# Two rings for the small statistics tiles of a hybrid encoder block

## The chip, the cores and the metric

The kernel runs on one core of a Trainium2 chip. The metric is the time of one execution on the device in microseconds; less is better. The tables and rows come from one profiled execution, taken by the hardware profiler: busy times of TensorE (PE, and PEld for its weight loads), VectorE (DVE), ScalarE (ACT), GpSimd (POOL) and the queue of SyncE (SP), which here issues DMAs only.

## The reference

One layer: an RMS norm and one input projection feed three token mixers (a gated linear recurrence, "HGRN"; a forgetting attention, "FoX"; a cross-attention into 256 memory tokens); their outputs are projected, gated, summed and projected again. Then follows a convolutional GLU. T = 1024 frames, width 1024, float32. What bears on the change is the query/key norm of the two attentions and the memory attention's softmax:

```python
def _rmsnorm(x, g):
    return xf * lax.rsqrt(jnp.mean(xf * xf, axis=-1, keepdims=True) + EPS) * g
...
    (hq, hf, hi, hg, fq, fk, fv, ff, mq, gate_logits) = jnp.split(z, pts, axis=-1)
...
def _fox_mixer(q, k, v, f_logit, f_bias, q_g, k_g):
    qh = _rmsnorm(q.reshape(B, T, FOX_HEADS, FOX_DH), q_g).transpose(0, 2, 1, 3)
    kh = _rmsnorm(k.reshape(B, T, FOX_HEADS, FOX_DH), k_g).transpose(0, 2, 1, 3)
...
def _memory_mixer(q, mem_kv, q_g, k_g):
    qh = _rmsnorm(q.reshape(B, T, MEM_HEADS, MEM_DH), q_g)
    s = jnp.einsum('bthd,bmhd->bhtm', qh, kh) * (MEM_DH ** -0.5)
    p = jax.nn.softmax(s, axis=-1)
    return jnp.einsum('bhtm,bmhd->bthd', p, vh).reshape(B, T, MEM_WIDTH)
```

## The kernel before, in words

A float32 matrix product is made of three matmuls on a split of each operand into a high and a low part (`mm3`, lines 122 to 124). Large products go by quarters with seven sub-products (Strassen's scheme, Winograd's form); their operands are named `B11`, `B12`, `B21`, `B22`, `T1` to `T4`, each with a high part `h` and a low part `l`.

The part that the change touches is the token-major projection, in five stages. Each is one `tm_unit` (stage 0 is `first_unit`): it takes a 1024 x 512 weight, splits it (`wh`, `wl`), multiplies in the order `B11`, `B21`, `T2`, `T1`, `T3`, `B22`, `T4`, and hands four output tiles `e` to a `put` function. A stage works in three pairs of PSUM banks, `pairs`: one of two `pp`, one of `pp` and `po`, one of two `lg`. Stage 0 makes the memory queries, stage 1 the recurrence's input, stage 2 queries and keys of FoX heads 0 to 3, stage 3 the FoX values, stage 4 queries and keys of heads 4 to 7. Then channel-major units follow (loads `ur`), woven with the FoX attention and the recurrence.

A query/key tile goes through `head_norm`: ACT squares it into the two PSUM banks of a pair (line 608), DVE sums per head (line 609), scales and adds epsilon (line 140), POOL raises to the power -1/2 (line 141), DVE multiplies the tile by it (line 612). Later PE transposes it into the same two banks (line 617), and ACT and DVE split the result into a key tile `ko` (lines 622 and 623), which SP stores. The statistics stand in a tile `r` of at most 16 columns.

Memory attention, `mem_attn`, runs in steps woven into stages 1 and 2 by a list, `slow`; each call of it has two logit steps and two value steps, eight calls in all, so sixteen of each. A logit step: PE logits into a `tr` bank, DVE maximum (line 667), its negative (668), ACT exponential with sum (670), DVE reciprocal (672), POOL scaling of `mpt` (674). The statistics stand in a tile `mst` of 8 columns. A value step: PE transposes of `mpt` (682), a split into `mph` (ACT, line 128) and `mpl` (DVE, line 136), PE products with the values, ACT copy `yo` (690), store. Of `tr` there are two banks, of `mpt` two buffers, of `mph`, `mpl` and `yo` one.

What sets the order: the code is traced in the order in which it is written; a scheduler then lays down one fixed order of instructions for each engine, by the order written, by what each needs, and by when buffers come free. `tm_sum` (line 445) adds weight quarters on POOL. All small tiles come from one place:

```python
def small(name, w):
    return cp.tile([P, 16], F32, tag="small", name=name, bufs=8)[:, :w]
```

This is one ring of eight buffers of 16 columns, with 109 tiles one after the other in it: the four `r` of each of stages 0, 2 and 4, `mst`, a small tile `fb` of the forget logits, the FoX softmax's `st`, and `eg` and `rr` of the recurrence.

Of the kernel before, what the change touches and what calls it, by code (L numbers as in the profile page):

```python
# [9 lines left out]
F32 = mybir.dt.float32  # L10
# [5 lines left out]
P = 128  # L16
# [53 lines left out]
def tile_block(ctx: ExitStack, tc: tile.TileContext, xT, x_rows, memT, mem_rows, vec, fbias, mats, hmask, w_ff, w_tm, w_cm,  # L70
# [4 lines left out]
    cp = ctx.enter_context(tc.tile_pool(name="cp", bufs=1))  # L75
# [22 lines left out]
    lbm, lbe0, lbe1 = (cp.tile([P, 4], F32, tag=t, name=t) for t in ("lbm", "lbe0", "lbe1"))  # L98

    def small(name, w):  # L100
        return cp.tile([P, 16], F32, tag="small", name=name, bufs=8)[:, :w]

    edge = ctx.enter_context(tc.tile_pool(name="edge", bufs=1, side="right"))
    edge.tile([P, EDGE], F32, tag="edge", name="edge")
# [2 lines left out]
    def col(i):  # L107
        return cv[:, i:i + 1]
# [29 lines left out]
    def rstd_small(out, ss, n):  # L138
        w = ss.shape[1]
        V.tensor_scalar(out, ss, 1.0 / n, EPS, ALU.mult, ALU.add)  # L140
        return G.tensor_tensor(out, out, mhalf[:, :w], ALU.pow)
# [427 lines left out]
    def forget_row():  # L569
        fb = small("fb", 2)[:16, :]  # L570
        V.memset(fb, 0.0)
        a, b = (half_tile(f"fr{i}")[:16, :] for i in range(2))
        for n in range(2):
            SP.dma_start(fb[8 * n:8 * n + 8, 0:1], fbias)
            SP.dma_start(a[8 * n:8 * n + 8, :], ffd[:, n * HB:(n + 1) * HB])
        V.tensor_scalar(a, a, fb[:, 0:1], None, ALU.add)
        S.activation(b, a, AF.Abs)
        S.activation(b, b, AF.Sigmoid)
        S.activation(b, b, AF.Ln)
        V.scalar_tensor_tensor(out=b, in0=a, scalar=0.0, in1=b, op0=ALU.min, op1=ALU.add)  # L580
        V.tensor_tensor_scan(a, ones[:16, :].to_broadcast([16, HB]), b, 0.0, ALU.mult, ALU.subtract)
        SP.dma_start(fb[8:16, 1:2], a[0:8, HB - 1:HB])
        V.tensor_scalar(a, a, fb[:, 1:2], None, ALU.add)
        for n in range(2):
            SP.dma_start(negFd[:, n * HB:(n + 1) * HB], a[8 * n:8 * n + 8, :])
# [15 lines left out]
    def head_norm(z, nh, bank):  # L601

        zz = [z[:, 2 * b:2 * b + 2, :].rearrange("p b (h d) -> p (b h) d", h=nh) for b in range(2)]
        r = small(f"r{nh}", 4 * nh)
        rs = [r[:, 2 * nh * b:2 * nh * (b + 1)] for b in range(2)]
        for b in range(2):
            sq = bank[b].rearrange("p (c d) -> p c d", c=2 * nh)
            S.activation(sq, zz[b], AF.Square)
            V.reduce_sum(rs[b], sq, axis=AX.X)
        rstd_small(r, r, 256 // nh)  # L610
        for b in range(2):
            V.tensor_mul(zz[b], zz[b], rs[b].unsqueeze(2).to_broadcast([P, 2 * nh, 256 // nh]))
# [12 lines left out]
    def put_fqk(pp):  # L625
        def put(c, n, z, bank):
            p = 2 * pp + c
            head_norm(z, 4, bank)

            def keys(what):  # L630
                t = ko_tile()
                turned(z, what, col(C_FK) if what == 0 else fqs, (t[:, 0, :], t[:, 1, :]), bank[what])
                SP.dma_start(kqd[p][what][:, :, n * HB:(n + 1) * HB], t.bitcast(F32))
            pending.append(lambda: keys(0))
            pending.append(lambda: keys(1))
        return put

    def put_mq(c, n, z, bank):
        head_norm(z, 2, bank)

        def queries(i):
            h = 2 * c + i
            t = ko_tile()
            turned(z, i, None, (t[:, 0, :], t[:, 1, :]), bank[i])
            SP.dma_start(mqd[h][:, :, n * HB:(n + 1) * HB], t.bitcast(F32))
            attn.append(mem_attn(h, n))
        pending.append(lambda: queries(0))
        pending.append(lambda: queries(1))

    def mem_attn(h, n):  # L650
# [8 lines left out]
        def logits(j):  # L659
            mqh, mql = tiles  # L660
            ps = ps_tr()
            pt = half_tile("mpt").rearrange("p (b m) -> p b m", b=2)
            st = small("mst", 8)
            for b in range(2):
                tsl = slice((2 * j + b) * P, (2 * j + b + 1) * P)
                mm3(ps[:, b * NM:(b + 1) * NM], mqh[:, tsl], mql[:, tsl], mem["mkh"][:, h, :], mem["mkl"][:, h, :], True, True)
            V.reduce_max(st[:, 0:2], ps.rearrange("p (b m) -> p b m", b=2), axis=AX.X)
            V.tensor_scalar(st[:, 2:4], st[:, 0:2], -1.0, None, ALU.mult)
            for b in range(2):
                S.activation(pt[:, b, :], ps[:, b * NM:(b + 1) * NM], AF.Exp, bias=st[:, 2 + b:3 + b],  # L670
                             accum_out=st[:, 4 + b:5 + b])
            V.reciprocal(st[:, 6:8], st[:, 4:6])
            for b in range(2):
                G.tensor_scalar(pt[:, b, :], pt[:, b, :], st[:, 6 + b:7 + b], 0.0, ALU.mult, ALU.add)
            pts.append(pt)
# [868 lines left out]
    for p in range(NF // 2):  # L1544
# [32 lines left out]
        for i in range(2):  # L1577
            f = 2 * p + i
            c = pq.tile([P, T], F32, tag="fc", name="fc", bufs=4)
            w = [col(C_CW + t * NF + f) for t in range(3)]  # L1580
# [88 lines left out]
    for a, b, own, first, c, n, sign, last, xq in (  # L1669
# [9 lines left out]
        for i, ks in enumerate(steps):  # L1679
# [11 lines left out]
            for m in range(4):  # L1691
                w = 256 if end and ks.stop == NP and m == 3 else HB
# [115 lines left out]
```

## Time and profile before

| | |
|---|---|
| median of 3 runs | 1710.43 us (1708.87 to 1712.0) |
| profiled execution, its own time | 1705.72 us |
| its span, first to last instruction | 1704.0 us |
| mean granted clock of TensorE | 0.994 |
| busy: PE, PEld | 1660.5 us (97%), 1417.7 us (83%) |
| busy: DVE, ACT, POOL | 1211.0 us (71%), 844.3 us (50%), 452.7 us (27%) |

Stages 0 to 4 lie between some 56 and 320 us of the span. A matmul counts as busy from its start to its modelled end, and matmuls overlap, so a busy time of PE that is the whole of a stretch means only that one was always in flight; the count of matmuls in the stretch (after the x) tells how fast they went. In timeline rows the columns are start in us, duration in us, engine, line, operation, written tile, read tiles, and in brackets the idle time before with what ended it.

### The profile page before, as it was taken

The page shows a single profiled execution, that of the slowest core. Times are in us where ns is not written, and L with a number is a line of the kernel's source. Part 1 is how long each engine was busy: PE and PEld are TensorE (multiplying, and loading weights), DVE is VectorE, ACT ScalarE, POOL GpSimd, SP SyncE. Part 2 cuts the span into 40 slices and gives each one's busy share as a digit, 9 for nine tenths or more (in the row PEclk, how much of TensorE's full clock was granted, in tenths as well). Part 3 has the DMA queues.
Part 4 walks back from the last instruction along what each step waited for, and adds up shares of the span by engine and source line. Part 5 has one row for each costly group of instructions (what it writes and reads, how often), then busy time and mean ns, then how long its engine had stood idle before and what let it go on. Part 6 is the DMA issues. An engine that isn't in the chain of part 4 may idle for free. (4 is left out here: it accounts for less than half of the span.)

```text
span 1704.0 us, 24944 instructions
## 1 busy us (share of the span) xinstructions
PE 1660.5 (97%) x8883; PEld 1417.7 (83%) x8883; DVE 1211.0 (71%) x2177; ACT 844.3 (50%) x1449; POOL 452.7 (27%) x482
## 2 busy tenths in 40 slices
PE   7999989999999999999999999999999999999999
PEld 5989979977788888888888788788888888888887
DVE  7874565668787676698766767787778878765654
ACT  7745544456666666556432356643434434343432
POOL 1433344365544444323011133311111111100000
PEclk9999989999999999999999999999999999999999
DMA  7352343365564444455966998866445445394772
GB/s 288 110 187 96 108 136 147 125 200 167 174 192 138 146 141 148 161 167 191 317 194 174 300 264 207 227 177 172 153 134 140 118 146 152 117 397 158 246 272 87
DMA packets 134749, 305.54 MB, mean 179 GB/s; under 512 B 14328, under 2 KB 31992, under 8 KB 133984
## 3 DMA queue, kind: packets, MB, share of 16 engines
q1 hardware_dynamic: 101008, 210.87, 36.5%
q0 software_dynamic: 24400, 78.39, 18.3%
q10 hardware_dynamic: 9216, 14.68, 2.3%
q8 instruction: 70, 1.15, 0.3%
q14 instruction: 55, 0.45, 0.1%
HBM read 223.21 MB, written 107.41 MB: 194 GB/s over the span
## 5 line engine op out<-in xcount | busy, mean ns | idle before, releaser
L1346 ACT CAST wh<-s 128x512 fp32r<-128x512 f32 x80 | 48.8, 619 | 113.2 <-PE pp L123 61.1
L128 ACT CAST dwh<-wr 128x1024 fp32r<-128x1024 f32 (+1 forms) x41 | 40.2, 980 | 115.7 <-PE tr L123 39.2
L730 ACT CAST uh<-ur 128x512 fp32r<-128x512 f32 x78 | 48.2, 618 | 77.5 <-PE pp L123 70.9
L1346 ACT CAST wh<-rw 128x512 fp32r<-128x512 f32 x70 | 43.0, 620 | 84.0 <-PE pp L123 45.5
L1470 POOL DMA_DIRECT2D rw<-in_w_up x40 | 22.3, 567 | 188.4 <-DVE wl L1347 142.4
L1045 POOL TENSOR_SCALAR pt<-pt,st 128x128 f32<-128x128 f32 (+3 forms) x64 | 56.8, 889 | 56.8 <-DVE st L1044 38.2
L136 DVE TENSOR_TENSOR dwl<-wr,dwh 128x1024 fp32r<-128x1024 f32 (+1 forms) x41 | 46.3, 1129 | 34.1 <-ACT dwh L128 33.3
L122 PE MATMUL pp<-B21h,uh 128*128 128x512 f32 x168 | 66.8, 400 | 3.8 <-DVE gt L895 2.6
L731 DVE TENSOR_TENSOR ul<-us,uh 128x512 fp32r<-128x512 f32 x72 | 55.2, 770 | 20.1 <-ACT uh L730 19.5
L1043 ACT ACTIVATE pt<-pt,st 128x128 f32<-128x128 f32 (+3 forms) x64 | 49.8, 778 | 39.1 <-DVE st L1040 33.6
L736 POOL TENSOR_TENSOR us<-ur 128x512 f32<-128x512 f32 x36 | 48.6, 1351 | 71.5 <-DMA ur<-in_w_cm 55.4
L731 DVE TENSOR_TENSOR ul<-ur,uh 128x512 fp32r<-128x512 f32 x78 | 60.8, 779 | 8.8 <-ACT uh L730 8.3
L124 PE MATMUL pp<-B21h,ul 128*128 128x512 f32 x168 | 66.3, 394 | 0.1
L123 PE MATMUL pp<-T2l,uh 128*128 128x512 f32 x168 | 66.3, 395 | 0.0
L122 PE MATMUL pp<-T2h,uh 128*128 128x512 f32 x168 | 66.2, 397 | 0.0
L123 PE MATMUL pp<-B21l,uh 128*128 128x512 f32 x168 | 66.0, 393 | 0.0
L124 PE MATMUL pp<-T2h,ul 128*128 128x512 f32 x168 | 65.9, 393 | 0.0
L736 POOL TENSOR_TENSOR us<-us,ur 128x512 f32<-128x512 f32 x36 | 50.7, 1409 | 38.1 <-issue 31.9
L730 ACT CAST uh<-us 128x512 fp32r<-128x512 f32 x72 | 43.9, 615 | 33.7 <-POOL us L736 17.9
L1347 DVE TENSOR_TENSOR wl<-rw,wh 128x512 fp32r<-128x512 f32 x70 | 47.0, 685 | 17.7 <-PE pp L124 14.9
L136 DVE TENSOR_TENSOR wl<-raw,wh 128x1024 fp32r<-128x1024 f32 x29 | 36.8, 1273 | 27.7 <-ACT wh L128 27.5
L1347 DVE TENSOR_TENSOR wl<-s,wh 128x512 fp32r<-128x512 f32 x80 | 54.5, 681 | 0.0
(721 smaller groups left out, 6157.6 us busy)
## 6 DMA issues: line engine op xcount, KB each, us to landing
rw<-in_w_up POOLq DMA_DIRECT2D x40, 512.0 KB, 4.8
ur<-in_w_cm SPq DMA_DIRECT2D x72, 256.0 KB, 3.5
sd<-in_w_dn POOLq DMA_DIRECT2D x30, 512.0 KB, 6.1
br<-yd SPq DMA_DIRECT2D x30, 512.0 KB, 4.6
gd<-uo ACTq DMA_DIRECT2D x48, 256.0 KB, 2.2
gt<-gd SPq DMA_DIRECT2D x48, 256.0 KB, 7.5
yd<-fc SPq DMA_DIRECT2D x44, 256.0 KB, 2.0
raw<-in_w_tm SPq DMA_DIRECT2D x20, 512.0 KB, 3.4
```

The costliest lines, as they stand in the source:

```text
L122: PE.matmul(ps, lh, rh, start=first, stop=False, skip_group_check=more)
L123: PE.matmul(ps, lh, rl, start=False, stop=False, skip_group_check=more)
L124: return PE.matmul(ps, ll, rh, start=False, stop=last, skip_group_check=more)
L128: S.copy(out, in_)
L136: return (sub or V).tensor_sub(l, src, h.bitcast(F32))
L730: marks["cast"] = S.copy(h, src)
L731: V.tensor_sub(l, src, h.bitcast(F32))
L736: G.tensor_add(t, a, b)
L1043: S.activation(pt[:, :ns], pt[:, :ns], AF.Exp, bias=st[:, 2:3], accum_out=st[:, 3:4])
L1045: G.tensor_scalar(pt[:, :ns], pt[:, :ns], st[:, 3:4], 0.0, ALU.mult, ALU.add)
L1346: late["cast"] = S.copy(h, src)
L1347: late["split"] = V.tensor_sub(l, src, h.bitcast(F32))
```

## The change

The ring `small` keeps its eight buffers, but of 8 columns instead of 16; the tiles `r` of the head norms get a ring of their own, `norm`, with four buffers of 16 columns. 8 x 16 columns are as many as 8 x 8 and 4 x 16, so what lies behind in memory stays where it is. No instruction is added or removed.

```diff
     def small(name, w):
-        return cp.tile([P, 16], F32, tag="small", name=name, bufs=8)[:, :w]
+        return cp.tile([P, 8], F32, tag="small", name=name, bufs=8)[:, :w]
...
     def head_norm(z, nh, bank):
 
         zz = [z[:, 2 * b:2 * b + 2, :].rearrange("p b (h d) -> p (b h) d", h=nh) for b in range(2)]
-        r = small(f"r{nh}", 4 * nh)
+        r = cp.tile([P, 16], F32, tag="norm", name=f"r{nh}", bufs=4)[:, :4 * nh]
```

The order of the engines differs from the middle of stage 2 to the start of stage 4. The four norms of stage 2 appear as `r_2062`, `r_2423`, `r_2558` and `r_2692`, in the order written. In the rows below a name stands for a tile without its buffer number.

PE at the end of stage 2, before: from the last `T4` product of the stage on there are 100 instructions of memory attention and of the transposes of `r_2062`'s and `r_2423`'s tiles ahead of the first `B11` product of stage 3. These stand 70 instructions into them:

```order
 L682 MATMUL tr<-ident,mpt 128x128
 L122 MATMUL tr<-mkh,mqh 128x256
 L123 MATMUL tr<-mkl,mqh 128x256
 L124 MATMUL tr<-mkh,mql 128x256
 L122 MATMUL tr<-mkh,mqh 128x256
 L123 MATMUL tr<-mkl,mqh 128x256
 L124 MATMUL tr<-mkh,mql 128x256
 L617 MATMUL pp<-ident,e 128x128 x4
 L682 MATMUL tr<-ident,mpt 128x128 x3
 L617 MATMUL pp<-ident,e 128x128 x4
```

The same place on PE after the change, from the last `T4` product of stage 2 to the first `B11` product of stage 3 (`mph` and `mvh` are memory attention):

```order
 L122 MATMUL lg<-wh,T4h 128x256
 L123 MATMUL lg<-wl,T4h 128x256
 L124 MATMUL lg<-wh,T4l 128x256
 L122 MATMUL tr<-mph,mvh 128x256
 L123 MATMUL tr<-mpl,mvh 128x256
 L124 MATMUL tr<-mph,mvl 128x256
 L122 MATMUL tr<-mph,mvh 128x256
 L123 MATMUL tr<-mpl,mvh 128x256
 L124 MATMUL tr<-mph,mvl 128x256
 L122 MATMUL pp<-wh,B11h 128x256
```

The transposes of `r_2423`'s tile moved ahead of the second half of `T4`, and of the 100 instructions six stand between the stages now; the others are spread over stage 2, stage 3 and the first product of stage 4.

DVE around the norm `r_2423`, before (`mst`, `mpl` are memory attention):

```order
 L672 RECIPROCAL mst<-mst 128x2
 L667 TENSOR_REDUCE mst<-tr 128x2
 L609 TENSOR_REDUCE r_2423<-pp 128x8 x2
 L668 TENSOR_SCALAR mst<-mst 128x2
 L136 TENSOR_TENSOR mpl<-tr,mph 128x512
 L140 TENSOR_SCALAR r_2423<-r_2423 128x16
 L672 RECIPROCAL mst<-mst 128x2
 L612 TENSOR_TENSOR e<-e,r_2423 128x512 x2
```

DVE around the same norm after the change (`e` from `lg` is the norm's own tile, being put together from the projection's banks):

```order
 L148 SCALAR_TENSOR_TENSOR e<-lg,e 128x512
 L672 RECIPROCAL mst<-mst 128x2
 L609 TENSOR_REDUCE r_2423<-pp 128x8
 L148 SCALAR_TENSOR_TENSOR e<-lg,e 128x512
 L136 TENSOR_TENSOR wl<-raw,wh 128x1024
 L609 TENSOR_REDUCE r_2423<-pp 128x8
 L140 TENSOR_SCALAR r_2423<-r_2423 128x16
 L136 TENSOR_TENSOR mpl<-tr,mph 128x512
```

The sums now stand right behind the halves of the tile that they are taken of. Before, fourteen of the sixteen `mst` reductions stood ahead of them; now eight do.

POOL in stages 2 and 3, the difference (power of a norm at line 141, softmax scalings at 674, weight sums at 445):

```order
 L674 TENSOR_SCALAR mpt<-mpt,mst 128x256 x2
 L445 TENSOR_TENSOR ws<-raw 128x512 x2
+L141 TENSOR_TENSOR r_2062<-r_2062,mhalf 128x16
 L674 TENSOR_SCALAR mpt<-mpt,mst 128x256 x6
 L445 TENSOR_TENSOR ws<-raw 128x512 x2
 L445 TENSOR_TENSOR ws<-ws,raw 128x512 x2
-L141 TENSOR_TENSOR r_2062<-r_2062,mhalf 128x16
-L674 TENSOR_SCALAR mpt<-mpt,mst 128x256 x10
 L141 TENSOR_TENSOR r_2423<-r_2423,mhalf 128x16
 L674 TENSOR_SCALAR mpt<-mpt,mst 128x256 x2
```

The power of `r_2062` moved ahead of the weight sums of stage 3 and of six scalings, that of `r_2423` ahead of ten scalings.

On SP, the stores of the first two key tiles of stage 2 (line 633) moved ahead of two loads of memory queries (line 657) and of the last weight load of stage 3 (line 213), and the four `ur` loads of the first channel-major unit (line 796) moved behind the eight stores of stage 3's values (line 700).

## The prediction

> **What bounds the kernel now.** I read the page first (busy times, then the slices), then busy time by stretches of 20 us, then the waits inside the one stretch that stood out, then the timeline of that stretch on each engine.
>
> ```profile
> span 1704.0 us, 24944 instructions
> PE 1660.5 (97%) x8883; PEld 1417.7 (83%) x8883; DVE 1211.0 (71%) x2177; ACT 844.3 (50%) x1449; POOL 452.7 (27%) x482
> ```
>
> TensorE is the bound: 43.5 us of 1704.0 are not PE. No change of buffers touches the matmuls, so the gain can only come from PE's idle time and from matmuls run at a low granted clock. The table by stretches (us, then busy time and count of PE, PEld, DVE, ACT, POOL, then granted clock) shows where these lie in the part the change concerns.
>
> ```profile
> 160.00:180.00 20.00, 20.00 (x170) 20.00 (x170) 9.71 (x14) 9.93 (x22) 7.00 (x9) 1.00 0.39 121
> 180.00:200.00 20.00, 20.00 (x170) 20.00 (x169) 11.58 (x21) 9.67 (x23) 10.88 (x10) 1.00 0.23 73
> 200.00:220.00 20.00, 14.69 (x102) 13.41 (x100) 10.40 (x21) 11.31 (x28) 3.87 (x8) 0.91 0.38 126
> 220.00:240.00 20.00, 13.31 (x91) 12.13 (x90) 12.34 (x27) 6.91 (x22) 11.12 (x9) 0.83 0.19 72
> 240.00:260.00 20.00, 20.00 (x170) 20.00 (x170) 11.58 (x16) 10.69 (x19) 8.31 (x7) 1.00 0.76 264
> 440.00:460.00 20.00, 17.16 (x76) 14.21 (x75) 15.16 (x30) 13.72 (x23) 9.41 (x9) 0.83 0.44 151
> ```
>
> Between 200 and 240 us PE ran 193 matmuls, where 20 us before and after hold 170 each. The timeline gives this hole its edges: the last projection matmul of stage 2 and the first of stage 3, with memory attention alone in between.
>
> ```profile
> 205.31 0.28 PE L124 MATMUL lg<-wh,T4l 128*128 128x256 f32 x1
> 205.43 0.60 PE L682 MATMUL tr<-ident,mpt 128*128 128x128 f32 x4
> ...
> 235.02 0.28 PE L124 MATMUL tr<-mkh,mql 128*128 128x256 f32 x1
> 235.14 0.28 PE L122 MATMUL pp<-wh,B11h 128*128 128x256 f32 x1
> ```
>
> Why does stage 3 start so late? Its first product writes `pairs[0]`, the banks in which `put_fqk` squares and transposes the second query/key tile. The norm of that tile (`r_2423`) goes like this:
>
> ```profile
> 208.96 0.66 ACT L608 ACTIVATE pp<-e 128x512 f32<-128x512 f32 x1
> 210.01 0.64 ACT L608 ACTIVATE pp<-e 128x512 f32<-128x512 f32 x1
> 222.22 0.69 DVE L667 TENSOR_REDUCE mst<-tr 128x2 f32<-128x512 f32 x1 [0.86 <-PE tr L124]
> 222.83 1.28 DVE L609 TENSOR_REDUCE r<-pp 128x8 f32<-128x512 f32 x2
> 224.94 2.91 POOL L141 TENSOR_TENSOR r<-r,mhalf 128x16 f32<-128x16 f32 x1 [2.55 <-DVE r L140]
> 227.83 1.90 POOL L674 TENSOR_SCALAR mpt<-mpt,mst 128x256 f32<-128x256 f32 x2
> 227.88 1.49 DVE L612 TENSOR_TENSOR e<-e,r 128x512 f32<-128x512 f32 x2 [2.38 <-POOL r L141]
> 230.45 1.05 PE L617 MATMUL pp<-ident,e 128*128 128x128 f32 x4
> ```
>
> The squares are done at 210.65, the sums start at 222.83: 12 us in which DVE had idle time and nothing was missing but the order. In the built order every `r` stands behind the `mst` tiles written before it: all these small tiles come from one ring, which hands them out in the order of the program, and `r_2423` is written after fourteen of the sixteen `mst`. The memory attention, a serial chain through single buffers, is behind; the norm waits its turn, and with it the projection.
>
> **The change, part by part.** No instruction is added or removed, only the order moves: the norms leave the ring that memory attention fills.
>
> *The hole.* Same view, cut at its edges:
>
> ```profile
> 145.23:205.43 60.20, 60.20 (x507) 60.03 (x506) 31.58 (x53) 32.97 (x68) 21.69 (x25) 1.00 0.32 104
> 205.43:235.14 29.71, 17.72 (x102) 15.25 (x101) 15.70 (x34) 15.64 (x42) 9.87 (x10) 0.83 0.22 76
> 235.14:276.00 40.86, 40.86 (x345) 40.86 (x344) 27.50 (x37) 19.11 (x33) 21.30 (x16) 1.00 0.60 216
> ```
>
> Beside it a row of PE costs 60.20/507 = 0.1187 us. The 102 in the hole must still run: 12.1 us. Removed: 29.71 - 12.1 = 17.6 us, of which 29.71 - 17.72 = 12.0 is idle and 5.6 the low clock (0.83) and the drained ends of lone matmuls. In the changed order the first `B11` matmul of stage 3 follows the last `T4` of stage 2 after only six attention matmuls, and the chain's remaining steps stand inside the products of stage 3 and the first of stage 4.
>
> *New waits inside stages 2 and 3.* PE is in order, so each woven attention step can stop a product. Bound from below: zero, since ten of the sixteen attention steps were already woven before the hole (their reductions, first fence), and from 145 to 205 us PE was full. Bound from above: what each such place waited in the hole, where nothing covered it (second fence: total, times, longest).
>
> ```profile
> L667 DVE TENSOR_REDUCE mst<-tr x10: 673/692/692, 119.1 to 200.4; 128x2 f32<-128x512 f32 x10
> ```
>
> ```profile
> PE tr L122 <- DVE mpl L136: 4.9, 5, 1.8
> PE tr L682 <- POOL mpt L674: 3.0, 1, 3.0
> PE tr L122 <- ACT yo L690: 1.9, 1, 1.9
> PE tr L122 <- ACT mpt L670: 1.9, 2, 1.0
> ```
>
> That is 11.7 us in 9 waits, 1.3 each. The steps most at risk are three where POOL's power (`r_2423`, `r_2558`, `r_2692`) stands right ahead of a softmax scaling. The scaling chain, from reduction to scaled tile, runs here:
>
> ```profile
> 210.12 0.68 DVE L667 TENSOR_REDUCE mst<-tr 128x2 f32<-128x512 f32 x1
> 212.44 0.94 POOL L674 TENSOR_SCALAR mpt<-mpt,mst 128x256 f32<-128x256 f32 x2 [7.74 <-DVE mst L672]
> ```
>
> So 3.3 us, some 0.3 for the logits to drain, and 2.9 for a power in front make 6.5. Between logits and transposes the changed order leaves 58, 71 and 59 rows of PE, at 0.1187 us 6.9, 8.4 and 7.0: it fits, barely. Two of them could slip by about half a microsecond, so I take 1.0 in all; it lies near the lower end, because the distances are of the size that held from 145 to 205.
>
> The row at 227.83 shows two scalings in 1.90 us beside DVE's two-input multiply, where the one at 212.44 took 0.94; if all three powers' scalings are slowed so, the chain is 7.5 and about 1.1 us of waits follow, still my term. The Trainium skill's GPSIMD Engine Reference, section Specifications, says GpSimd shares its SBUF interfaces with VectorE and contends with instructions of two SBUF inputs; that speaks against moving norms in among scalings, and the trace agrees in this one pair of rows.
>
> *What else moves.* The norm sums and multiplies on DVE, the squares and key/query scalings on ACT: same count, now beside PE work. On SP the first key stores of stage 2 go ahead of two query loads and of stage 3's last weight load, which POOL's weight sums wait for, and `r_2423`'s power now stands right behind those sums:
>
> ```profile
> 186.11 0.38 SPq L213 DMA_DIRECT2D raw<-in_w_tm  x1
> 190.80 3.39 POOL L445 TENSOR_TENSOR ws<-raw 128x512 f32<-128x512 f32 x2 [1.72 <-DMA raw<-in_w_tm]
> 194.15 2.55 POOL L445 TENSOR_TENSOR ws<-ws,raw 128x512 f32<-128x512 f32 x2
> ```
>
> The stores are due near 180 and take some 1.2 us to issue, so the load should not slip. The sums end at 196.7, a power behind them at 199.6, the scaling at 200.5 to 201.5; the transposes of that tile stand 39 rows ahead of stage 2's last matmul, near 200.8: again 0 to 0.7 us, inside my 1.0. The loads of unit 0 (`ur`) go behind stage 3's stores, since their pool needs memory attention's tiles, now free only in stage 4:
>
> ```profile
> L796 SPq DMA_DIRECT2D ur<-in_w_cm x8: 338/582/689, 252.6 to 336.8; - x8
> DMA to landing us min/median/max: 5.2/7.9/8.0
> ```
>
> Stage 4 has some 358 rows (42 us) of PE work before unit 0 starts; a landing of 7.9 us is covered. ACT's casts of these loads stand ahead of stage 4's first norm squares, though: a load 8 us late would hold those, and there the order has 103 rows (12.2 us) from product to transposes. I cost it at nothing. After stage 4 the order is the same but shifted.
>
> *Sum.* 17.6 - 1.0 = 16.6 us. The profiled execution took 1705.72 us (span 1704.0, 1.7 around it) and would become 1689.1. It stands 4.7 below the median of the runs shown, 1710.43; against that median the forecast is 1693.8 us. 0.2%, about what a measurement of this kernel can tell from no change, is 3.4 us here.
>
> **The rivals.**
>
> *POOL's powers hold the scalings.* For it: the 3.0 us wait above, at 225.9, is a scaling behind a power. If all three cost that, 3 x 3.0 = 9.0 us come back: 17.6 - 9.0 = 8.6, 1701.8 us. The clock may be lost too: in the hole 5.6 us went beside 12.0 of idle, 0.47 per us, which makes it 13.2 and 1706.0. Against: the distances above, and the hole had no cover at all.
>
> These clock losses came with single waits no longer than 3.0 us:
>
> ```profile
> 215.75 0.41 PE L123 MATMUL tr<-mpl,mvh 128*128 128x256 f32 x1
> ...
> 229.38 0.41 PE L123 MATMUL tr<-mkl,mqh 128*128 128x256 f32 x1
> ```
>
> (0.41 us against 0.28 at full clock.) The Trainium skill's TensorE: Matmul & The Clock Gate, section HAM oscillation, gives as its abstract rule no idle gap over about 3.4 us; by that rule waits of 3 us leave the clock alone and this rival ends at 1701.8. The trace disagrees, so I keep 1706.0 as well.
>
> *Slower: every woven step stops PE.* From stage 3's first product on, the order has 6 logit, 7 transpose and 7 value groups, 20 places. At 1.3 us each they cost 26 us, with the clock's 0.47 38: 1710.4 - 17.6 + 38 = 1731. It decides from 17.6/1.47 = 12 us, 0.6 per place. Against: the same weave before 205 us cost nothing.
>
> *The wait moves on.* Stage 3 starts early but stops on something else (ACT held by the late loads of unit 0, or the chain's end before `ur` is free), and all is given back: 1710. For it only that six attention steps move into a stretch that had two; against, DVE and ACT are busy under 70% there.
>
> **How the numbers follow.** Forecast 0.78, around 1693.8 (1690 to 1698). Powers 0.11, 1701.8 to 1706.0. Slower 0.05. Wait moves on 0.06. The range: below, 17.6 with no new wait and the low-clock stretch at 440 to 460 (0.83, some 3.4 us) gone by the shift gives 1689; above, the powers' lower price, 1702. Faster by over 0.2%: 0.78 and the powers' 0.11 make 0.89; same 0.06; slower 0.05.
>
> **What would show it.** Right: no stretch of 20 us between 145 and 280 with PE under 19 or a clock under 0.95; `B11` of stage 3 starting near 206; squares and sums of `r_2423` within 2 us of each other; everything from the FoX loop on shifted by 16 to 17 us. Wrong: waits of PE on `mpt` (POOL) or `mpl` (DVE) between 175 and 270 adding to more than 3 us; a clock dip in stage 3; waits on `ur`.

## The result

The change made the kernel faster: 1692.7 us (median of 4 runs, 1691.21 to 1693.93) against 1709.65 us (median of 4, 1707.78 to 1712.0), a ratio of 0.9896, 95% interval 0.9881 to 0.991. That is 17.0 us (15.4 to 20.3 by the interval), where 16.6 were forecast.

The head of the page of the kernel after (span; busy time, share and count of each engine):

```profile
span 1690.1 us, 24934 instructions
PE 1657.3 (98%) x8883; PEld 1416.6 (84%) x8883; DVE 1211.8 (72%) x2177; ACT 843.6 (50%) x1449; POOL 455.5 (27%) x482
```

Its busy times by stretches (columns as in the prediction):

```profile
180.00:200.00 20.00, 20.00 (x170) 20.00 (x169) 12.87 (x22) 10.60 (x25) 11.04 (x10) 1.00 0.36 126
200.00:220.00 20.00, 19.99 (x170) 19.79 (x170) 16.57 (x28) 13.11 (x28) 12.25 (x9) 1.00 0.44 156
220.00:240.00 20.00, 20.00 (x170) 20.00 (x169) 10.84 (x19) 10.70 (x26) 7.40 (x10) 1.00 0.65 214
240.00:260.00 20.00, 20.00 (x171) 20.00 (x170) 13.97 (x20) 10.13 (x23) 8.40 (x8) 1.00 0.38 144
...
360.00:380.00 20.00, 18.12 (x91) 15.47 (x90) 15.53 (x44) 12.98 (x21) 9.59 (x11) 0.91 0.80 243
420.00:440.00 20.00, 17.60 (x87) 14.67 (x86) 14.67 (x35) 13.51 (x23) 9.15 (x9) 0.91 0.52 180
```

The hole is gone. Where 193 matmuls ran between 200 and 240 us, 340 do now, at a granted clock of 1.00. The last two rows lie in the FoX loop, in which nothing was meant to change; before, that loop had one dip, to 0.83 at 440 to 460.

The stage edge on PE, and the transposes of a softmax tile just ahead of it and behind it (of the four, the first and the third need the first of the tile's two scalings, the second and the fourth the second scaling):

```profile
201.64 0.27 PE L682 MATMUL tr<-ident,mpt 128*128 128x128 f32 x1
...
202.10 0.49 PE L682 MATMUL tr<-ident,mpt 128*128 128x128 f32 x3
...
206.06 0.28 PE L124 MATMUL lg<-wh,T4l 128*128 128x256 f32 x1
...
206.90 0.28 PE L122 MATMUL pp<-wh,B11h 128*128 128x256 f32 x1
...
209.30 0.27 PE L682 MATMUL tr<-ident,mpt 128*128 128x128 f32 x1
...
209.65 0.28 PE L123 MATMUL pp<-wl,B11h 128*128 128x256 f32 x1
209.94 0.55 PE L682 MATMUL tr<-ident,mpt 128*128 128x128 f32 x3
```

Stage 3 starts at 206.90 instead of 235.14. The norm of `r_2423` on DVE and on POOL; the last two rows of DVE are the multiply of the next norm and a weight split, the last two of POOL the power of that norm and two scalings beside the multiply and the split:

```profile
189.31 0.69 DVE L609 TENSOR_REDUCE r<-pp 128x8 f32<-128x512 f32 x1 [0.33 <-ACT pp L608]
193.13 0.68 DVE L609 TENSOR_REDUCE r<-pp 128x8 f32<-128x512 f32 x1
...
206.99 1.50 DVE L612 TENSOR_TENSOR e<-e,r 128x512 f32<-128x512 f32 x2 [0.23 <-POOL r L141]
208.40 1.21 DVE L136 TENSOR_TENSOR wl<-ws,wh 128x1024 fp32r<-128x1024 f32 x1
```

```profile
194.31 2.55 POOL L445 TENSOR_TENSOR ws<-ws,raw 128x512 f32<-128x512 f32 x2
196.82 2.92 POOL L141 TENSOR_TENSOR r<-r,mhalf 128x16 f32<-128x16 f32 x1
199.73 1.89 POOL L674 TENSOR_SCALAR mpt<-mpt,mst 128x256 f32<-128x256 f32 x2
204.05 2.90 POOL L141 TENSOR_TENSOR r<-r,mhalf 128x16 f32<-128x16 f32 x1 [2.44 <-DVE r L140]
206.94 2.94 POOL L674 TENSOR_SCALAR mpt<-mpt,mst 128x256 f32<-128x256 f32 x2
```

The first sum waits only for its square; before, it came 12 us after the squares. The squares, on ACT:

```profile
188.68 0.60 ACT L608 ACTIVATE pp<-e 128x512 f32<-128x512 f32 x1
191.46 0.61 ACT L608 ACTIVATE pp<-e 128x512 f32<-128x512 f32 x1
```

To place the gain I cut the program at three landmarks: the norms' transposes (617), the FoX loop's transposes (1057) and a step of the convolutional GLU (1584), each with shortest, median and longest ns, then first and last start. Before, then after:

```profile
L617 PE MATMUL pp<-ident,e x60: 270/272/421, 72.3 to 327.5; 128*128 128x128 f32 x60
L1057 PE MATMUL tr<-ident,pt x128: 270/272/297, 362.4 to 702.2; 128*128 128x128 f32 x128
L1584 ACT ACTIVATE fc<-fc x22: 1056/1062/1066, 1096.9 to 1481.9; 128x1024 f32<-128x1024 f32 x22
```

```profile
L617 PE MATMUL pp<-ident,e x60: 270/272/299, 72.0 to 309.5; 128*128 128x128 f32 x60
L1057 PE MATMUL tr<-ident,pt x128: 270/272/421, 344.7 to 683.7; 128*128 128x128 f32 x128
L1584 ACT ACTIVATE fc<-fc x22: 1055/1062/1069, 1083.0 to 1468.1; 128x1024 f32<-128x1024 f32 x22
```

| part, us | before | after | difference |
|---|---|---|---|
| stages: first 617 to first 1057 | 290.1 | 272.7 | -17.4 |
| FoX loop: first to last 1057 | 339.8 | 339.0 | -0.8 |
| last 1057 to first 1584 | 394.7 | 399.3 | +4.6 |
| GLU: first to last 1584 | 385.0 | 385.1 | +0.1 |

So the stages gained what the runs gained. The 4.6 us given back in the third part is not the change's: over twelve kernels of this study that have the same order there, that part took 394.7 to 402.2 us, and the profile of before is the shortest of them. That execution was also some 4 us under the median of its runs. Most of the difference is the granted clock (the third number from the end). The part has two dips after the change, and one before:

```profile
940.00:960.00 20.00, 17.59 (x70) 14.04 (x70) 15.91 (x22) 7.02 (x9) 2.20 (x3) 0.91 1.06 303
1050.00:1070.00 20.00, 17.04 (x79) 14.22 (x78) 13.62 (x27) 14.64 (x28) 11.07 (x15) 0.83 0.93 235
```

```profile
1060.00:1080.00 20.00, 16.91 (x80) 13.90 (x78) 14.51 (x25) 15.23 (x29) 13.14 (x17) 0.91 1.01 220
```

By these rows 20 x (0.09 + 0.17) = 5.2 us of clock are lost after, and 20 x 0.09 = 1.8 us before: 3.4 of the 4.6 us. Why the clock dips more often there was not looked into.

### The profile page after: what moved, and what is told of

Same layout as the page of the kernel before. It is cut to its first block, busy times and chain, and to the rows that moved or that the text cites. A ratio compares the mean times of both kernels' runs of the same rounds, so it can differ in the third digit from the quotient of the medians.

```text
span 1690.1 us, 24934 instructions
## 1 busy us (share of the span) xinstructions
PE 1657.3 (98%) x8883; PEld 1416.6 (84%) x8883; DVE 1211.8 (72%) x2177; ACT 843.6 (50%) x1449; POOL 455.5 (27%) x482
## 4 chain that ended last, share of the span: by engine, by line
PE 52%; DMA 2%; DVE 1%; issue 0%; ACT 0%; POOL 0%; DVEq 0%; POOLq 0%
PE pp L122 10%; PE pp L123 10%; PE pp L124 10%; PE lg L124 4%; PE lg L122 4%; PE lg L123 4%; PE tr L124 2%; PE tr L122 2%; PE tr L123 2%; DMA gt<-gd 1%; PE po L122 1%; PE po L124 1%; PE po L123 1%; PE lg L1175 1%; DMA r<-sq 0%
```

## The experiments

The theory: one ring hands its buffers out in the order in which tiles are written, so the norms stood behind a softmax chain that they have nothing to do with. The rivals: the ring was too small; the place of tiles in memory; each norm that is freed brings a share. The parts below are those of the table above. `BASE`, in several edits, is the width of a spare tile: it takes up what a ring gains or gives up, so that everything behind keeps its place in memory.

### Is it the number of buffers?

`one10`, from the kernel before:

```diff
-EDGE, BASE = 120, 56
+EDGE, BASE = 120, 24
-        return cp.tile([P, 16], F32, tag="small", name=name, bufs=8)[:, :w]
+        return cp.tile([P, 16], F32, tag="small", name=name, bufs=10)[:, :w]
```

> One ring as before, but of ten buffers instead of eight; everything behind it in memory stays where it is, and the order of instructions on every engine is that of before. Theory (the norms wait because one ring hands out its tiles in the order written, not because it is small): the hole of about 30 us with some 100 matmuls of attention between the last T4 of stage 2 and the first B11 of stage 3 stays; ratio 1.000 to the kernel before, 1706 to 1713 us. Rival (eight buffers were too few): a gain that grows with the buffers, 1693 to 1704 us.

Ratio 0.9985, 0.9968 to 1.0003; the hole is there, from 207.12 to 237.68 us, with the same 100 matmuls in it, and the engines' order through the stages is that of the kernel before:

```profile
207.24:237.68 30.44, 19.46 (x103) 16.93 (x102) 15.71 (x34) 15.61 (x42) 9.85 (x10) 0.72 0.21 74
```

Two more buffers do nothing that can be told from no change. A ring of many more was not tried.

`norm1`, from the kernel after:

```diff
-EDGE, BASE = 120, 56
+EDGE, BASE = 120, 104
-        r = cp.tile([P, 16], F32, tag="norm", name=f"r{nh}", bufs=4)[:, :4 * nh]
+        r = cp.tile([P, 16], F32, tag="norm", name=f"r{nh}", bufs=1)[:, :4 * nh]
```

> The kernel after with one buffer in the norms' ring instead of four, placement in memory kept. Theory (what matters is that the norms are out of the other ring, not the number of buffers): the gain of the kernel after, 1690 to 1696 us, no hole. Rival (the four further buffers matter): half of the gain or less, 1700 to 1710 us, with the norms of stage 2 waiting for each other's buffer.

A miss by the total: ratio 1.001, 0.9991 to 1.003, no gain. But two stretches of its profile tell where it went, the woven stages and the FoX loop:

```profile
145.00:280.00 135.00, 135.00 (x1134) 134.76 (x1134) 86.09 (x133) 77.68 (x156) 62.24 (x55) 1.00 0.41 143
345.10:702.50 357.40, 343.94 (x1797) 289.55 (x1796) 247.52 (x715) 213.22 (x418) 164.25 (x183) 0.98 0.47 147
```

There is no hole, and the stages take 273.4 us, as after. The loss is in the FoX loop, 357 us instead of 339, with 13.5 us of idle PE instead of 7.5 (kernel after: 331.73 of 339.20 busy) and with 35 matmuls more between its landmarks (1797 against 1762). Loop and the part behind it together take 754.5 us, against 738.3 in the kernel after. With one buffer the order of the loop's instructions comes out differently on every engine, though the loop has none of the norms. `norm2` has two buffers (BASE 88), and the order of the kernel after on every engine.

> The kernel after with two buffers in the norms' ring instead of four (place in memory kept), which leaves the order of instructions on every engine as it is in the kernel after. With one buffer the stages had no hole either, but the order of the FoX loop came out another way and the loop took 357 us instead of 339. Theory (the number of buffers does not matter, the loop's order took the gain of the one-buffer kernel): 1690 to 1696 us, FoX loop 338 to 341 us. Rival (the buffers themselves matter): 1699 to 1710 us.

Ratio 0.988, 0.9863 to 0.9898. Its FoX loop:

```profile
345.60:685.80 340.20, 331.02 (x1762) 279.19 (x1762) 248.45 (x712) 211.68 (x415) 164.51 (x182) 0.99 0.49 152
```

The number of buffers in the norms' ring is not what brings the gain, and for the stages one is enough. That the one-buffer kernel lost through the loop's order rests on the two profiles; which instruction of that order costs the time was not pursued.

### Which norms?

Four kernels take only some of stage 2's norms out of the shared ring of the kernel before (BASE 40, one further buffer):

```diff
+    calls = []
     def head_norm(z, nh, bank):
...
-        r = small(f"r{nh}", 4 * nh)
+        calls.append(nh)
+        own = nh == 4 and calls.count(4) in (1,)
+        r = cp.tile([P, 16], F32, tag="norm", name=f"r{nh}")[:, :16] if own else small(f"r{nh}", 4 * nh)
```

The list is (1,) in `p1_first`, (1, 2) in `p12_two`, (3, 4) in `p34_late` and (2, 3, 4) in `p234_three`. Lines behind this place are 4 higher.

> The kernel before, with only the first norm of stage 2 in a ring of its own. The second, whose squares fill the banks that stage 3's first product writes, still stands behind fourteen of sixteen softmax tiles. Theory (the one wait that counts is that norm's): the hole stays at about 100 matmuls and 30 us, 1706 to 1712 us, no change. Rival (each of the four norms of stage 2 that leaves the ring brings its share, a quarter of 17 us): 1703 to 1707 us.

Ratio 1.0002, 0.9986 to 1.0018: the theory's value; a quarter of the gain is excluded. The hole, from 207.73 to 237.59 us, still holds 100 matmuls.

> The kernel before, with the first and the second norm of stage 2 in a ring of their own; the third and fourth stay with the softmax tiles. Theory: stage 3's first product starts at once, but its next, B21, needs the banks of the third norm's tile, which still waits in the shared ring; the hole moves behind the first product and holds 79 matmuls of attention instead of 100. At the 17.6 us that the hole of 100 lost, 0.176 each, it loses 13.9, a gain of 3.7 us: 1704 to 1708 us. Rival (the second norm alone was the cause): the full gain, 1692 to 1696 us. Rival (each norm a quarter): half the gain, 1699 to 1703 us.

Ratio 0.9997, 0.9982 to 1.0012, a gain of at most 3 us: every number missed, the theory's the least. The hole did move behind stage 3's first products:

```profile
208.96:223.14 14.18, 14.18 (x121) 14.18 (x120) 6.75 (x10) 6.96 (x17) 3.48 (x4) 1.00 0.42 136
223.14:248.10 24.96, 15.01 (x81) 12.41 (x80) 13.14 (x29) 10.67 (x29) 14.10 (x14) 0.78 0.23 82
```

It loses 24.96 - 81 x 0.1187 = 15.3 us, not 13.9. PE waits 5.9 us there for scalings; 3.9 of them are one wait for a scaling behind a power of a norm, where the hole before had 3.0 of that. It is the longest, on PE:

```profile
243.22 0.48 PE L686 MATMUL tr<-ident,mpt 128*128 128x128 f32 x1 [3.92 <-POOL mpt L678]
```

> The kernel before, with only the third and the fourth norm of stage 2 in a ring of their own. The second stays in the shared ring, so stage 3's first product still waits, and the work of the two freed norms now comes ahead of it: 127 matmuls between the last T4 of stage 2 and the first B11 of stage 3 instead of 100. Theory (the time goes with the matmuls that stand alone in the hole, 0.176 us each): 4 to 5 us slower than before, 1712 to 1717 us. Rival (a share for each norm moved): 8 us faster, 1699 to 1704 us. Rival (the further rows are transposes that would run anyway): no change.

Ratio 1.0003, 0.999 to 1.0015: no change. The hole:

```profile
207.90:241.51 33.61, 23.36 (x130) 19.51 (x128) 19.05 (x39) 16.45 (x44) 15.70 (x15) 0.80 0.20 67
```

It is longer by 3.9 us, with 28 more matmuls, and loses 33.61 - 130 x 0.1187 = 18.2 us against 17.6. The price of 0.176 us for a matmul, on which the expectation stood, is wrong: the loss did not grow with the rows, as the second rival had it: they are transposes that would run anyway, and the idle time in the hole is 10.3 us instead of 12.0. What a hole loses goes rather with the attention steps left in it: this one holds five softmax reductions, as before, and a sixth that starts 0.3 us before its end.

> The kernel before, with the second, third and fourth norm of stage 2 in a ring of their own; only the first stays with the softmax tiles. Between the last T4 of stage 2 and the first B11 of stage 3 stand 50 matmuls of other work instead of 100, and no further hole behind. Theory (the loss goes with the attention steps that stand alone there, half of them left): 7 to 10 us faster than before, 1699 to 1704 us. Rival (the loss is in the waits on scalings behind a power, and one norm left in the ring is enough for it): 1705 to 1711 us. Rival (three of four norms freed is as good as four): 1691 to 1695 us.

Ratio 0.9938, 0.9918 to 0.9958: 7 to 14 us faster, as the theory had it. Its hole:

```profile
205.44:221.07 15.63, 9.96 (x53) 8.87 (x52) 11.29 (x22) 9.90 (x23) 8.35 (x6) 0.67 0.34 120
```

It holds two softmax reductions instead of five, and loses 15.63 - 53 x 0.1187 = 9.3 us; the stages take 284.7 us. So the last norm in the shared ring still costs half, and the dose fits: nothing for one freed that nobody waits for, nothing measurable for two, half for three, all for four.

### Does it take a second ring?

`b_steps2` and `b_steps4` are the kernel before, one ring of eight, with this constant at 2 or at 4; `a_steps4` is the kernel after with 4:

```diff
-STAGE_STEPS = 3
+STAGE_STEPS = 2
```

> The kernel before, one ring of eight for all small tiles, with one constant changed: two attention steps are written between the parts of a stage instead of three. Then the norms of stage 2 are written behind 6, 10, 10 and 11 softmax tiles instead of 10, 14, 14 and 15 or so, and the built order has no hole. Theory (the order written decides, a second ring is only one way to mend it): as fast as the kernel after, 1690 to 1698 us. Rival (the separate ring or the place of the tiles in memory makes the gain): 1706 to 1713 us.

Ratio 0.992, 0.9898 to 0.9942; 1695.31 us. Its stretch of the woven stages:

```profile
145.00:280.00 135.00, 132.57 (x1112) 132.17 (x1112) 82.51 (x132) 72.57 (x153) 56.99 (x53) 1.00 0.41 144
```

No hole, with the old ring. Nothing was changed but the places in the program at which attention steps are written, and most of the gain is there: the separate ring is not needed for it. The 2.4 us of idle PE in it, all at 140 to 160, are about what its stages lack to the kernel after (275.5 us against 272.7). The constant moves the attention's instructions together with its tiles, so this run alone does not show that it is the ring that ties the norms to them. The kernel after shows it (the same places in the program, another ring), and so does `a_steps4` below.

> The kernel before, one ring, with four attention steps written between the parts of a stage instead of three: the norms stand behind 12, 16, 16 and 16 softmax tiles, and the hole holds 116 matmuls instead of 100. Theory (0.176 us lost for each matmul of the hole): 2.8 us slower than before, 1710 to 1716 us. Rival (the attention's length sets the stretch and the number written does not matter): within 0.2% of before.

Ratio 1.0053, 1.0036 to 1.0071: 9 us slower. The direction is the theory's, the size three times what was expected. Its hole, and what PE waited for in it:

```profile
204.61:245.07 40.46, 24.38 (x119) 19.85 (x117) 21.76 (x46) 17.32 (x46) 16.64 (x14) 0.70 0.18 59
```

```profile
PE tr L682 <- POOL mpt L674: 5.9, 3, 2.8
PE tr L122 <- DVE mpl L136: 4.7, 2, 3.3
PE tr L122 <- ACT yo L690: 2.5, 4, 1.1
PE pp L617 <- DVE e L612: 2.4, 2, 1.5
```

It loses 40.46 - 119 x 0.1187 = 26.3 us, 8.7 more than before, which is the 9 us of the runs. Six reductions are in it instead of five, and PE waits three times for a scaling instead of once.

> The kernel after with four attention steps written between the parts of a stage instead of three, the FoX loop's order unchanged: with its norms in their own ring the attention may be written as early as it likes. Theory (with the norms free, earlier attention can only fill TensorE's idle time in stage 1, 1.5 us between 100 and 140 us, and opens no hole): 1690 to 1694 us, the same as the kernel after or 1 to 2 us less, while the same constant cost the kernel with one ring 9 us. Rival (the hole comes back, since the number of steps set it): 1705 to 1715 us.

Ratio 0.988, 0.9865 to 0.9894. The same constant that cost one ring 9 us costs two rings nothing: the attention is written still earlier, and the norms do not wait for it. From 100 to 140 us PE is now full:

```profile
100.00:140.00 40.00, 40.00 (x308) 35.96 (x308) 25.23 (x38) 17.36 (x35) 13.65 (x13) 1.00 0.56 190
```

The kernel after has 38.45 busy there. These 1.5 us are not seen in the time: `norm2`, with the kernel after's order and on the same chip, has the same ratio. No version here beats the kernel after by what can be measured.

### How near to the edge, and does the place matter?

`pow2`, from the kernel after (lines behind are 2 higher):

```diff
         rstd_small(r, r, 256 // nh)
+        if nh == 4:
+            G.tensor_tensor(cp.tile([P, 16], F32, tag="norm", name="again", bufs=4), r, mhalf, ALU.pow)
```

> The kernel after, in which GpSimd raises each norm's statistics to the power a second time, into a spare tile, right behind the first time: 2.9 us more in front of each softmax scaling that follows a power, in stages 0, 2 and 4. Theory (in the kernel after the scalings behind a power come out with almost nothing to spare): TensorE waits for the scaled tiles of memory attention at up to three places, 1 to 3 us each, 1694 to 1702 us, with rows of waits on mpt. Rival (there is slack that the trace does not show, or the wait is taken up later): same as the kernel after, 1691 to 1694 us.

Ratio 0.9971, 0.9956 to 0.9987, 1706.25 us: slower than expected by either, and for another reason. The woven stages and the FoX loop:

```profile
145.00:280.00 135.00, 135.00 (x1135) 134.84 (x1134) 84.67 (x132) 77.69 (x158) 71.80 (x59) 1.00 0.42 145
344.80:693.70 348.90, 338.36 (x1788) 285.70 (x1787) 255.28 (x716) 214.29 (x417) 159.59 (x182) 0.99 0.48 150
```

POOL is busy 71.80 us in the stages, where the kernel after has 61.33, and PE waits for nothing: the scheduler laid down another order, in which the further powers are covered. So it did not test the spare time of a fixed order. What it lost is again in the loop, 349 us, whose order came out differently.

`a_shift` is the kernel after with `EDGE, BASE = 120, 24`, its order the same.

> The kernel after, with everything behind the small tiles moved by 32 columns in memory; the order of every engine unchanged. Theory (place in memory plays no part in the gain): 1690 to 1696 us. Rival (part of the gain is where tiles lie): a change of more than 3 us from the kernel after.

Ratio 0.9964, 0.995 to 0.9979; 1704.03 us: the rival's result. The stages are those of the kernel after (271.2 us), so the hole's removal has nothing to do with place. The loss is in the GLU, which takes 396.1 us from its first to its last landmark, where every other kernel here takes 385.0 or 385.1; another 2.4 us are lost behind it. 350 us of the GLU, in the kernel after and then in this one:

```profile
1110.00:1460.00 350.00, 350.00 (x1545) 289.79 (x1545) 278.93 (x414) 146.03 (x222) 46.96 (x75) 1.00 0.49 140
```

```profile
1110.00:1460.00 350.00, 350.00 (x1502) 282.00 (x1501) 271.10 (x404) 141.04 (x215) 45.84 (x73) 1.00 0.48 138
```

A matmul comes every 350/1502 = 233 ns instead of 227, at full clock and with no wait. The kernel before has 1545 in the same stretch, as after: the change left the place alone, and gained or lost nothing by it.

## Why the prediction was right

- *The hole, 17.6 us.* The stages are 17.4 us shorter. Stage 3's `B11` starts at 206.90 (near 206 was said), and between 145 and 280 us no stretch of 20 us has PE under 19 or a clock under 0.95. Squares and sums stand together: the sums start 0.03 and 1.1 us after the squares end.
- *The cause.* Shown by `b_steps2` (the written order alone brings most of it), `one10` (two more buffers bring nothing), `a_steps4` (with the norms in their own ring the written order no longer matters) and the dose of `p1_first` and `p234_three`.
- *New waits, 1.0 us.* Too high: no wait of PE on `mpt` or `mpl` is listed between 145 and 280 us, and 17.6 - 17.4 leaves 0.2. That remainder is not known so closely, since the stages took 274.2 us in `norm2` and 271.2 in `a_shift`, in the same order as the 272.7 of the kernel after. "It fits, barely" was right. Behind the first power the second scaling is done at 199.73 + 1.89 = 201.62, and the transposes that need it start at 202.10, 0.5 us later. Behind the second it is done at 206.94 + 2.94 = 209.88, and they start at 209.94, 0.29 us after the matmul ahead of them instead of 0.12: a slip of some 0.2 us.
- *Scalings slowed beside DVE's two-input multiply.* Seen behind two of the three powers: 1.89 us for two scalings, as in the pair shown before, and 2.94, where two alone take 0.94. The second pair fell into the spare time but for the slip above. Its second scaling is the slowest of all, 1958 ns, 1.48 us over the 480 of one alone; it ran beside the rest of the multiplies (to 208.49) and the whole of the weight split behind them (208.40 to 209.61, two inputs in SBUF as well), and ended 0.27 us after the split. The prediction counted the multiply alone. All 32 scalings in one row (shortest, median and longest ns), and the slowest:

```profile
L674 POOL TENSOR_SCALAR mpt<-mpt,mst x32: 475/480/1958, 121.8 to 255.7; 128x256 f32<-128x256 f32 x32
207.92 1.96 POOL L674 TENSOR_SCALAR mpt<-mpt,mst 128x256 f32<-128x256 f32 x1
```

  The Trainium skill's SBUF — State Buffer, section "SBUF: two separate sides", says that a DVE instruction with two SBUF inputs and a GpSimd instruction that reads SBUF exclude each other for a whole instruction instead of sharing; these numbers agree.
- *`ur` late, SP's stores.* Nothing, as costed: the loads start at 264.8 us and PE waits for nothing in stage 4.
- *The shift.* 16 to 17 us was said from the FoX loop on; it is 17.7 at its start, 18.5 at its end and 13.9 from the GLU on. What did not come is the last term of the range's low end: the clock dip at 440 to 460 did not go with the shift but became two of 0.91, and the loop is 0.8 us shorter, not 3.4. The drop to 13.9 is the part behind the loop, 4.6 us longer, of which 3.4 are clock. So the profiled execution took 1691.85 us where 1689.1 were forecast, while the median came within 1.1 us of its forecast.
- *The rivals.* Powers before scalings do cost PE 2.7 to 3.9 us each where attention stands alone (`p12_two`, `p234_three`), as that rival priced them; woven among products they cost the slip of 0.2 us. Neither the stop at every woven step nor the wait on the channel-major units occurred.
- *The clock.* In the hole of `p234_three` the clock is 0.67, with no wait of PE over 2.7 us. The abstract rule of the Trainium skill's TensorE: Matmul & The Clock Gate, section "HAM oscillation", no idle gap over about 3.4 us, does not foretell that loss; this case's measurements decide against leaning on it.

## What to carry to other kernels

A ring of buffers shared by unrelated chains turns the order in which the program writes their tiles into an order between the chains. It shows in a trace as an instruction whose input is done and whose engine idles, behind instructions of the other chain; a ring of its own for the shorter chain mends it, and so can writing the longer chain later. Price such a hole by the serial steps left in it, not by its matmuls: the holes here lost 3.5 to 4.7 us for each softmax reduction in them (9.3 for two, 15.3 for four, 17.6 and 18.2 for five, 26.3 for six), a rough price. And before judging a variant by its total, compare order and placement elsewhere: here each changed the time by 10 to 18 us in parts that the edit did not touch.

## What was not expected of the hardware

32 columns (128 bytes a partition) of shift slowed the GLU's matmuls from one every 227 ns to one every 233, 11 us in all, at a granted clock of 1.00, with the same instructions in the same order. Which operand's place does it was not tried. The FoX loop took 339, 349 and 357 us in three orders, with 1762, 1788 and 1797 matmuls between its landmarks.
